# Seven products for both halves of the down projection, with weight sums added by DMA and results added to x from PSUM

## The chip, the cores and the metric

One Trainium2 chip, one of its cores. The time is that of one execution on the device, in microseconds (us); lower is better. Three executions of the kernel before took 1492.73, 1492.98 and 1493.35 us, median 1492.98 us.

## What is computed

The layer takes 256 tokens of width 2048 in float32. The change touches its MLP only:

```python
hm = rmsnorm(x, g_mlp[i])
x = x + jnp.square(jax.nn.relu(hm @ w_up[i])) @ w_down[i]
```

`w_up` is 2048 x 8192 and `w_down` is 8192 x 2048. Ahead of the MLP stand the input projections, two attention branches and an output projection; behind it stands a gated embedding with one more 2048 x 2048 product.

## The kernel before

**Precision.** Every weight tile is split into a high part `wh` (written by ACT, L82) and a low part `wl` (the rest, by DVE, L83), both fp32r. One split pair covers 128x1024 numbers. A product of an activation part and a weight chunk is three matmuls: high by high, high by low, low by high. In the up projection the weights are the stationary operand and both parts of the activations stream past them, so a step there is one matmul of 512 columns for `wh` and one of 256 for `wl` (L526, L527).

**The MLP's stages.** The hidden width is cut into eight slabs of 1024. `up_units` makes the hidden activations of one slab (eight 1 MB loads, each two split pairs, four calls of `hidden`). While it makes slab s + 1, the down projection of slab s runs beside it. `together` interleaves the streams of units: it gives each unit of a stream a due place between 0 and 1 and takes them in that order. A scheduler then orders the instructions on each engine; each engine runs its own in that order and waits at the first that isn't ready.

**The down projection.** For a slab, `w_down` is two halves `n` of the output columns, and each half is four quarters `(i, j)` of 512 rows by 512 columns, 1 MB each. Rows of tokens come in two tiles `tt` of 128. `plain_units` (half 1 of slabs 0 to 6, both halves of slab 7) forms the 2 x 2 block product with eight block products: four quarters, each split once (8 split pairs), 96 matmuls of 512 columns, collected in PSUM banks `m` and added to x by `add_rows` (L448). `fast_units` (half 0 of slabs 0 to 6) uses seven block products of sums (Strassen's scheme in Winograd's form): the sums of activations are made in `hidden` (L508 to L511), the sums of weights on DVE over the loaded quarters (L560, 128x2048), each of the seven products splits its own weights (14 split pairs) and needs 84 matmuls (L546, L548, L550) into banks `s`. Three partial results are copied out of PSUM by ACT (`keep`, L556) and added to x later (L560, L614); the rest go by `add_rows`. x itself lives in SBUF as `xr`.

**Buffers and queues.** `raw` (loads), `wh` and `wl` have three buffers each. The quarters of a fast half have four buffers of their own (`quart`). All weight loads are issued by SP (SyncE), in order; each waits there for its buffer. POOL (GpSimd) has no work in the MLP. `later(us, fn)` puts off an emission until the planner's clock, which `advance` moves, has gone on by so much.

Of the kernel before, what the change touches and what calls it, by code (L numbers as in the profile page):

```python
# [22 lines left out]
DH = 128  # L23
# [36 lines left out]
def layer_kernel(ctx: ExitStack, tc: tile.TileContext, xt, xm, pt, gains, qkg, cst,  # L60
                 wa, wba, wbb, wo, wup, wdn, wpg, wpp, out):
    nc = tc.nc
    const = ctx.enter_context(tc.tile_pool(name="const", bufs=1))
# [4 lines left out]
    work = mixers.enter_context(tc.tile_pool(name="work", bufs=2))  # L68
# [43 lines left out]
    def later(us, fn, *args):  # L112

        pending.append((clock[0] + us, len(pending), fn, args))
# [47 lines left out]

    cs = work.tile([P, C_END], F32, tag="cs", name="cs", bufs=1)
    idt = const.tile([P, P], F32, name="idt")
    gq = const.tile([P, 2, DH], F32, name="gq")
    ident = idt
    ones = cs[:, C_ONES:C_ONES + P]
    tri = cs[:, C_TRI:C_TRI + P]
# [53 lines left out]
    PIECE = 512  # L222
    xr = []
# [54 lines left out]
    for n, (dst, gain) in enumerate(((qT, gq[:, 0, :]), (kT, gq[:, 1, :]))):  # L278
        for g in range(2):
            if rt is None:  # L280
                ps = group_m(range(4), h, first_weights)
# [107 lines left out]

    yb = new_acts("yb", NH)  # L390
    sb_pair = []
    tri_r = const.tile([P, P], F32R, name="tri_r")
    ones_r = const.tile([P, P], F32R, name="ones_r")
    nc.scalar.activation(tri_r, tri, AF.Copy)
    nc.scalar.activation(ones_r, ones, AF.Copy)
    ga = [block([P, D], F32, f"ga{tt}") for tt in range(2)]
# [10 lines left out]
    for g in range(4):  # L407
        ps = group_m([wba[g, c] for c in range(2)], ya)
# [66 lines left out]

    rms = []
    r2 = const.tile([P, 2], F32, name="r2")
    r2n = const.tile([P, 1], F32, name="r2n")

    def mlp_norm():  # L480
        rms.append(rows_norm(ss1, "rt1", mw))
        nc.vector.tensor_tensor(r2, rms[0], rms[0], op=ALU.mult)
        nc.vector.tensor_scalar(r2n, r2[:, 0:1], -1.0, None, op0=ALU.mult)

    later(14, mlp_norm)
    mlp = ExitStack()
    hid = mlp.enter_context(tc.tile_pool(name="hid", bufs=7))
    mw = mlp.enter_context(tc.tile_pool(name="mw", bufs=2))
    ps2 = mlp.enter_context(tc.tile_pool(name="ps2", bufs=1, space=PSUM))
    FAST = [(s, 0) for s in range(7)]  # L490

    def bank2(tag, bufs=1):
        return ps2.tile([P, 512], F32, tag=tag, name=f"ps_{tag}", bufs=bufs)
# [44 lines left out]
    def fast_units(s, n, f):  # L538

        def product(ps, a, b, start):
            for p0 in range(2):
                for i, (wh, wl) in enumerate(split_weights(b[:, 2 * p0:2 * p0 + 2, :], 2, PIECE)):
                    k = 2 * p0 + i
                    nc.tensor.matmul(ps, f[k][:, 0, a, :], wh, start=start and k == 0, stop=False,  # L546
                                     skip_group_check=not start)
                    nc.tensor.matmul(ps, f[k][:, 0, a, :], wl, start=False, stop=False,  # L548
                                     skip_group_check=not start)
                    nc.tensor.matmul(ps, f[k][:, 1, a, :], wh, start=False, stop=k == 3,  # L550
                                     skip_group_check=not start)
                    advance(0.68)

        def keep(ps, tt):
            t = mw.tile([P, PIECE], F32, tag="cp", name="cp", bufs=5)
            nc.scalar.activation(t, ps, AF.Copy, scale=r2[:, tt:tt + 1])  # L556
            return t

        def add(a, b):
            nc.vector.tensor_tensor(a, a, b, op=ALU.add)  # L560

        b = {}
        for i, j in ((0, 0), (0, 1), (1, 1), (1, 0)):
            b[i, j] = mw.tile([P, 4, PIECE], F32, tag="quart", name="quart", bufs=4)
            nc.sync.dma_start(b[i, j].rearrange("p k c -> p (k c)"), wdn[s, n, i, j])
        c1, c2 = 2 * n * PIECE, (2 * n + 1) * PIECE
        left = [slice(c1, c1 + PIECE), slice(c2, c2 + PIECE)]
        waiting = []

        def sum_later(a, b):  # L570

            waiting.append((a, b))
            later(2, sums)

        def sums():
            while waiting:
                add(*waiting.pop(0))

        px = bank2("s", 4)
        product(px, A11, b[0, 0], True)  # L580
        s1 = keep(px, 1)
        sum_later(b[0, 0], b[0, 1])
        yield
        sums()
        pz = bank2("s", 4)
        product(pz, S1, b[0, 0], True)
        z0 = keep(pz, 0)
        sum_later(b[0, 0], b[1, 1])
        yield
        sums()  # L590
        product(px, S2, b[0, 0], False)
        s2 = keep(px, 1)
        sum_later(b[0, 0], b[1, 0])
        yield
        sums()
        pw = bank2("s", 4)
        product(pw, A22, b[0, 0], True)
        w0 = keep(pw, 0)
        sum_later(b[0, 1], b[1, 1])
        yield  # L600
        py = bank2("s", 4)
        product(py, A12, b[1, 0], True)
        add(xr[1][:, left[0]], s1)
        add_rows(1, c1, py, r2[:, 1:2])
        yield
        sums()
        product(px, S3, b[0, 1], False)
        add(xr[0][:, left[0]], w0)
        add_rows(0, c1, px, r2[:, 0:1])
        add(xr[0][:, left[1]], z0)  # L610
        add_rows(0, c2, px, r2n)
        yield
        product(pz, S4, b[1, 1], False)
        nc.vector.tensor_tensor(xr[1][:, left[1]], xr[1][:, left[1]], s2, op=ALU.subtract)  # L614
        add_rows(1, c2, pz, r2[:, 1:2])
        yield

    def plain_units(s, n, u):
# [33 lines left out]
    em = []  # L652

    def embedding_units():
        em.extend(mw.tile([P, D], F32, tag="quart", name=f"em{tt}", bufs=4) for tt in range(2))
        praw = mw.tile([P, 2, T], F32, tag="hs", name="praw", bufs=2)
        nc.sync.dma_start(praw, pt)
        pr = hid.tile([P, 2, 2, T], F32R, tag="hid", name="pr")
        split(pr[:, 0], pr[:, 1], praw)
        for n in range(2):  # L660
            raw = load(wpp[n], 2, 1024)
            for j in range(2):
                ps = [bank2("mm", 2) for _ in range(2)]
                parts = split_weights(raw[:, :, j * PIECE:(j + 1) * PIECE], 2, PIECE)
                for kt, (wh, wl) in enumerate(parts):
                    for tt in range(2):
                        t = slice(tt * P, (tt + 1) * P)
# [12 lines left out]
    def finished(g):  # L680
        if g == 0:
            h3.extend(new_acts("h3_", pool=blk))
        for tt in range(2):
            squares_rows(tt, g, ss2, mw.tile([P, PIECE], F32, tag="cp", name="junk", bufs=5))
        later(3, turn, g, h3, 2)

    def last_units(u):
# [8 lines left out]
    for s in range(7):  # L696
        hids.append([])
        streams = [(0.5, 16, up_units(s + 1, hids[s + 1]))]
        for n in range(2):
            if (s, n) in FAST:  # L700
                streams.append((0.3, 7, fast_units(s, n, hids[s])))
            else:
                streams.append((0.75, 8, plain_units(s, n, hids[s])))
        together(*streams)
# [4 lines left out]
    def gate_out(g, tt, ps, c0, n):  # L709

        a, c = g * PIECE + c0, slice(g * PIECE + c0, g * PIECE + c0 + n)
        o = mw.tile([P, n], F32, tag="cp", name="o", bufs=5)
        nc.scalar.activation(o, ps[:, c0:c0 + n], AF.Sigmoid, scale=rms[1][:, tt:tt + 1])
        nc.vector.tensor_tensor(o, o, em[tt][:, c], op=ALU.mult)
        nc.vector.tensor_tensor(o, o, xr[tt][:, c], op=ALU.add)
        nc.sync.dma_start(out[tt, :, c], o)
# [78 lines left out]
```

## Time and profile before

| | |
|---|---|
| median of 3 runs | 1492.98 us |
| the profiled execution, its own time | 1492.93 us |
| its span in the profile | 1491.1 us |
| slabs 0 to 6 with their down projections | about 716 to 1338 us of the span |
| PE busy, share of the span | 99% |
| DVE / ACT busy, share of the span | 67% / 56% |
| POOL busy | 42.4 us, all ahead of the MLP |
| read from DRAM | 275.83 MB |

The profiled execution is within 0.05 us of the median. In the profile, a row of the timeline gives the start in us from the span's start, the duration, the engine, the line, the operation and its tiles; "x2" is two of them merged; in brackets stands how long the engine was idle ahead of it and what ended that. Ends of matmuls are modelled, so the distance between starts is the better measure of a matmul's cost.

### The profile page before, as it was taken

The numbers are of one execution on the slowest core, as the hardware profiler recorded it, in microseconds if no ns is written. First come the engines' busy times: TensorE is split into PE (matmuls) and PEld (weight loads), VectorE is DVE, ScalarE is ACT, GpSimd is POOL, SyncE is SP. The second block draws the span as 40 slices with busy tenths as digits, with TensorE's granted clock in tenths as the row PEclk, the third lists the DMA queues.
The fourth block names the chain that finished last, engine by engine and source line by source line (L and its number), as shares of the span: only waits on it lengthen the run. The fifth ranks groups of instructions, "written<-read, shape, count | busy, mean of one in ns | idle before, by whom it ended". The sixth has DMA issues, their size and how long they took to land.

```text
span 1491.1 us, 17831 instructions
## 1 busy us (share of the span) xinstructions
PE 1470.8 (99%) x6960; PEld 1210.2 (81%) x6960; DVE 1000.4 (67%) x1209; ACT 840.3 (56%) x1084; POOL 42.4 (3%) x60
## 2 busy tenths in 40 slices
PE   7999999999999999999999999999999999999998
PEld 5888888888888888888787887878888787878886
DVE  5775555456555555556878879788787878765654
ACT  7444555488834444546655656656565655656543
POOL 0442000000000000000000000000000000000000
PEclk9999999999999999999999999999999999999999
DMA  8555544544455555557455464645546465444563
GB/s 330 174 196 193 175 155 159 194 169 170 169 182 190 193 185 186 194 178 302 141 198 198 170 226 140 228 170 191 204 155 239 143 208 191 159 146 154 201 221 111
DMA packets 40549, 279.09 MB, mean 187 GB/s; under 512 B 4624, under 2 KB 5136, under 8 KB 7312
## 3 DMA queue, kind: packets, MB, share of 16 engines
q1 hardware_dynamic: 40320, 277.92, 53.5%
q8 instruction: 54, 0.88, 0.2%
q14 instruction: 31, 0.25, 0.0%
q10 hardware_dynamic: 144, 0.02, 0.0%
HBM read 275.83 MB, written 2.10 MB: 186 GB/s over the span
## 4 chain that ended last, share of the span: by engine, by line
PE 92%; DVE 3%; issue 2%; DMA 1%; ACT 1%; SPq 0%; DVEq 0%; ACTq 0%
PE ps_mm L137 13%; PE ps_mm L139 13%; PE ps_mm L526 13%; PE ps_mm L138 13%; PE ps_mm L527 7%; PE ps_m L629 4%; PE ps_m L630 4%; PE ps_m L628 3%; PE ps_s L548 3%; PE ps_s L546 2%; PE ps_s L550 2%; PE ps_s L526 2%; DVE wl L83 2%; DMA raw<-in_wa 1%; ACT wh L82 1%
## 5 line engine op out<-in xcount | busy, mean ns | idle before, releaser
L83 DVE TENSOR_TENSOR wl<-raw,wh 128x1024 fp32r<-128x1024 f32 (+1 forms) x462 | 563.5, 1228 | 341.3 <-ACT wh L82 337.8
L82 ACT ACTIVATE wh<-raw 128x1024 fp32r<-128x1024 f32 (+1 forms) x462 | 485.3, 1054 | 404.2 <-PE ps_mm L139 222.8
L526 PE MATMUL ps_mm<-h,wh 128*128 128x512 f32 x896 | 321.3, 398 | 0.0
L137 PE MATMUL ps_mm<-wh,h 128*128 128x512 f32 x640 | 255.8, 400 | 5.5 <-ACT wh L82 5.5
L527 PE MATMUL ps_mm<-h,wl 128*128 128x256 f32 x896 | 251.8, 281 | 0.4
L138 PE MATMUL ps_mm<-wl,h 128*128 128x512 f32 x640 | 251.2, 393 | 0.6 <-DVE wl L83 0.5
L139 PE MATMUL ps_mm<-wh,h 128*128 128x512 f32 x640 | 251.0, 392 | 0.0
L526 PEld LDWEIGHTS ps_mm<-h,wh 128*128 128x128 f32 x896 | 168.3, 188 | 40.8 <-ACT wh L82 2.3
L83 DVE TENSOR_TENSOR wl<-quart,wh 128x1024 fp32r<-128x1024 f32 x98 | 120.1, 1225 | 83.3 <-ACT wh L82 83.2
L527 PEld LDWEIGHTS ps_mm<-h,wl 128*128 128x128 f32 x896 | 169.0, 189 | 8.2 <-DVE wl L83 3.2
L82 ACT ACTIVATE wh<-quart 128x1024 fp32r<-128x1024 f32 x98 | 104.0, 1061 | 123.2 <-PE ps_mm L526 87.0
L137 PEld LDWEIGHTS ps_mm<-wh,h 128*128 128x128 f32 x640 | 121.0, 189 | 31.7 <-ACT wh L82 8.1
L138 PEld LDWEIGHTS ps_mm<-wl,h 128*128 128x128 f32 x640 | 121.3, 189 | 26.8 <-DVE wl L83 2.6
L139 PEld LDWEIGHTS ps_mm<-wh,h 128*128 128x128 f32 x640 | 121.0, 189 | 25.8
L629 PE MATMUL ps_m<-wl,u 128*128 128x512 f32 x256 | 101.8, 397 | 4.1 <-DVE wl L83 4.0
L630 PE MATMUL ps_m<-wh,u 128*128 128x512 f32 x256 | 100.0, 391 | 0.0
L628 PE MATMUL ps_m<-wh,u 128*128 128x512 f32 x256 | 97.9, 392 | 1.6 <-DVE xr L448 1.6
L548 PE MATMUL ps_s<-wl,u 128*128 128x512 f32 x196 | 80.2, 409 | 0.0
L546 PE MATMUL ps_s<-wh,u 128*128 128x512 f32 x196 | 78.6, 401 | 0.0
L550 PE MATMUL ps_s<-wh,u 128*128 128x512 f32 x196 | 76.7, 392 | 0.0
L560 DVE TENSOR_TENSOR quart<-quart 128x2048 f32<-128x2048 f32 x28 | 64.1, 2289 | 0.5
L629 PEld LDWEIGHTS ps_m<-wl,u 128*128 128x128 f32 x256 | 48.1, 188 | 18.1 <-DVE wl L83 9.2
(204 smaller groups left out, 1826.0 us busy)
## 6 DMA issues: line engine op xcount, KB each, us to landing
raw<-in_wa SPq DMA_DIRECT2D x79, 1024.0 KB, 4.8
raw<-in_wup SPq DMA_DIRECT2D x64, 1024.0 KB, 4.8
raw<-in_wdn SPq DMA_DIRECT2D x36, 1024.0 KB, 4.8
quart<-in_wdn SPq DMA_DIRECT2D x28, 1024.0 KB, 4.8
raw<-in_wo SPq DMA_DIRECT2D x16, 1024.0 KB, 4.8
raw<-in_wpg SPq DMA_DIRECT2D x16, 1024.0 KB, 4.8
raw<-in_wba SPq DMA_DIRECT2D x8, 1024.0 KB, 4.8
raw<-in_wbb SPq DMA_DIRECT2D x8, 1024.0 KB, 4.8
```

Of the source, the lines that this page charges most:

```text
L82: nc.scalar.activation(hi, src, AF.Copy)
L83: nc.vector.tensor_tensor(lo, src, hi.bitcast(F32), op=ALU.subtract)
L137: nc.tensor.matmul(ps[tt], lhs[kt][:, 0, t], wh, start=kt == 0, stop=False)
L138: nc.tensor.matmul(ps[tt], lhs[kt][:, 0, t], wl, start=False, stop=False)
L139: nc.tensor.matmul(ps[tt], lhs[kt][:, 1, t], wh, start=False, stop=kt == last)
L526: nc.tensor.matmul(ps, wh, flat(h2[kt]), start=kt == 0, stop=False)
L527: nc.tensor.matmul(ps[:, :T], wl, h2[kt][:, 0, :], start=False, stop=kt == DT - 1)
L546: nc.tensor.matmul(ps, f[k][:, 0, a, :], wh, start=start and k == 0, stop=False, skip_group_check=not start)
L548: nc.tensor.matmul(ps, f[k][:, 0, a, :], wl, start=False, stop=False, skip_group_check=not start)
L628: nc.tensor.matmul(ps[tt], u[k][:, 0, a, :], wh, start=i + k == 0, stop=False)
L629: nc.tensor.matmul(ps[tt], u[k][:, 0, a, :], wl, start=False, stop=False)
L630: nc.tensor.matmul(ps[tt], u[k][:, 1, a, :], wh, start=False, stop=last)
```

## The change

- Half 1 of slabs 0 to 6 is also done by `fast_units`, so all 14 halves of these slabs take seven products. The two halves' streams stand at places 0.25 and 0.75 of a unit.
- In `fast_units` a half has one tile `chain` (three buffers) that holds quarter (0,0) and then grows by (0,1), (1,1) and (1,0). The first two sums are made by an accumulating DMA from DRAM that POOL issues (`add_loaded`, two DMAs of 512 KB per sum); the third is a DVE sum with a freshly loaded quarter (`last_sum`). A tile `right` (two buffers) holds (0,1) and gets (1,1) added on DVE. The two products with a plain quarter load it into `raw`.
- The order of the products is new. Nothing is copied out of PSUM: each product's bank is added to x by `add_rows` straight from PSUM, eight times per half, put off by 0.6 (once 2.1) on the planner's clock. Two of the seven products use banks `m`.
- Space: `gq`, `tri_r` and `ones_r` move to a pool that is closed ahead of the MLP; `cp` goes from five to two buffers and serves scratch and the last output only; the embedding's tiles `em` use the buffers of `right`.

```diff
-    r2n = const.tile([P, 1], F32, name="r2n")
+    r2n = const.tile([P, 2], F32, name="r2n")
...
-    FAST = [(s, 0) for s in range(7)]
+    FAST = [(s, n) for s in range(7) for n in range(2)]
...
-        def keep(ps, tt):
-            t = mw.tile([P, PIECE], F32, tag="cp", name="cp", bufs=5)
-            nc.scalar.activation(t, ps, AF.Copy, scale=r2[:, tt:tt + 1])
-            return t
+        def quarter(tag, bufs, i, j):
+            q = mw.tile([P, 4, PIECE], F32, tag=tag, name=tag, bufs=bufs)
+            nc.sync.dma_start(q.rearrange("p k c -> p (k c)"), wdn[s, n, i, j])
+            return q
+
+        def add_loaded(q, i, j):
+
+            for k in range(0, 4, 2):
+                nc.gpsimd.dma_start(q[:, k:k + 2, :].rearrange("p k c -> p (k c)"),
+                                    wdn[s, n, i, j, :, k * PIECE:(k + 2) * PIECE],
+                                    accum_op=ALU.add)
...
+        def last_sum():
+            add(chain, load(wdn[s, n, 1, 0], 4, PIECE))
...
+        chain = quarter("chain", 3, 0, 0)
         px = bank2("s", 4)
-        product(px, A11, b[0, 0], True)
-        s1 = keep(px, 1)
-        sum_later(b[0, 0], b[0, 1])
+        product(px, A11, chain, True)
+        add_loaded(chain, 0, 1)
+        later(0.6, add_rows, 1, c1, px, r2[:, 1:2])
         yield
-        sums()
+        py = bank2("m", 2)
+        product(py, A12, load(wdn[s, n, 1, 0], 4, PIECE), True)
+        later(0.6, add_rows, 1, c1, py, r2[:, 1:2])
+        yield
         pz = bank2("s", 4)
-        product(pz, S1, b[0, 0], True)
-        z0 = keep(pz, 0)
-        sum_later(b[0, 0], b[1, 1])
+        product(pz, S1, chain, True)
+        add_loaded(chain, 1, 1)
+        later(0.6, add_rows, 0, c2, pz, r2[:, 0:1])
+        right = quarter("right", 2, 0, 1)
         yield
...
+        b11 = load(wdn[s, n, 1, 1], 4, PIECE)
+        product(pz, S4, b11, False)
+        later(0.6, add_rows, 1, c2, pz, r2[:, 1:2])
+        later(2, add, right, b11)
         yield
...
+        product(px, S2, chain, False)
+        later(0.6, add_rows, 1, c2, px, r2n[:, 1:2])
+        later(6, last_sum)
         yield
...
+        pw = bank2("m", 2)
+        product(pw, A22, chain, True)
+        later(0.6, add_rows, 0, c1, pw, r2[:, 0:1])
         yield
...
+        product(px, S3, right, False)
+        later(0.6, add_rows, 0, c1, px, r2[:, 0:1])
+        later(2.1, add_rows, 0, c2, px, r2n[:, 0:1])
         yield
...
-                streams.append((0.3, 7, fast_units(s, n, hids[s])))
+                streams.append((0.25 + 0.5 * n, 7, fast_units(s, n, hids[s])))
```

How the order moves, first on DVE, in the middle of a slab, at a weight sum. Before, a sum (L560) of two loaded quarters stands between the splits of one product and those of the next (`quart_6979` is quarter (0,0), `cp` a copied result):

```order
L83 TENSOR_TENSOR wl_7093<-quart_6979,wh_7092 128x1024
L560 TENSOR_TENSOR quart_6979<-quart_6979,quart_6983 128x2048
L83 TENSOR_TENSOR wl_7151<-raw_7148,wh_7150 128x1024
L83 TENSOR_TENSOR wl_7155<-raw_7148,wh_7154 128x1024
L83 TENSOR_TENSOR wl_7175<-quart_6979,wh_7174 128x1024
L533 TENSOR_TENSOR hs_6951<-ps_mm_7054,ev_7121 128x256
L560 TENSOR_TENSOR xr0_247<-xr0_247,cp_7102 128x512
```

With the change (L568 is the sum, `raw_7171` the load of a product with a plain quarter, `raw_7320` quarter (1,1), which is loaded into the buffer that `raw_7171` had):

```order
L83 TENSOR_TENSOR wl_7184<-raw_7171,wh_7183 128x1024
L83 TENSOR_TENSOR wl_7198<-raw_7195,wh_7197 128x1024
L533 TENSOR_TENSOR hs_6991<-ps_mm_7089,ev_7157 128x256
L83 TENSOR_TENSOR wl_7202<-raw_7195,wh_7201 128x1024
L448 SCALAR_TENSOR_TENSOR xr1_248<-ps_m_7170,r2_5040,xr1_248 128x512
L83 TENSOR_TENSOR wl_7224<-chain_7019,wh_7223 128x1024
L508 TENSOR_TENSOR hr_7161<-hr_7161 128x128
L509 TENSOR_TENSOR hr_7161<-hr_7161 128x128
L568 TENSOR_TENSOR right_7245<-right_7245,raw_7320 128x2048
```

The sum now reads a tile whose load starts seven rows earlier, and an addition from PSUM (L448) stands among the splits.

The second place is SP's queue of loads in the same slab. Before, loads of the up projection (`in_wup`) stand with those of the plain half and of the four `quart` tiles:

```order
L91 DMA raw_7381<-in_wdn 128x2048
L91 DMA raw_7427<-in_wup 128x2048
L565 DMA quart_7707<-in_wdn 128x2048
L91 DMA raw_7520<-in_wup 128x2048
L91 DMA raw_7565<-in_wdn 128x2048
L565 DMA quart_7709<-in_wdn 128x2048
```

With the change, from the load of `raw_7171` to that of `raw_7582`; the tiles of L91 share three buffers in this order:

```order
L91 DMA raw_7171<-in_wdn 128x2048
L91 DMA raw_7195<-in_wup 128x2048
L91 DMA raw_7293<-in_wup 128x2048
L91 DMA raw_7320<-in_wdn 128x2048
L91 DMA raw_7375<-in_wup 128x2048
L91 DMA raw_7401<-in_wdn 128x2048
L91 DMA raw_7465<-in_wup 128x2048
L91 DMA raw_7516<-in_wdn 128x2048
L91 DMA raw_7568<-in_wup 128x2048
L91 DMA raw_7582<-in_wdn 128x2048
```

Where `quart` tiles with buffers of their own stood, quarters now go through the three `raw` buffers, alternating with the up projection's loads.

## Rows read from the trace of the kernel before

**Rows 1.** The page: busy time of each engine, and TensorE's granted clock in 40 slices.

```profile
PE 1470.8 (99%) x6960; PEld 1210.2 (81%) x6960; DVE 1000.4 (67%) x1209; ACT 840.3 (56%) x1084; POOL 42.4 (3%) x60
...
PEclk9999999999999999999999999999999999999999
```

**Rows 2.** Timeline of DVE: the same instruction in two neighbouring slabs.

```profile
810.06 0.29 DVE L510 TENSOR_TENSOR hr<-hr 128x128 f32<-128x128 f32 x1
...
898.85 0.28 DVE L510 TENSOR_TENSOR hr<-hr 128x128 f32<-128x128 f32 x1
```

**Rows 3.** Timeline of PE: twelve 512-column matmuls in a row, then eight up-projection pairs.

```profile
1382.62 0.39 PE L628 MATMUL ps_s<-wh,u 128*128 128x512 f32 x1
...
1385.34 0.39 PE L668 MATMUL ps_mm<-wh,pr 128*128 128x512 f32 x1
...
709.95 0.39 PE L526 MATMUL ps_s<-h,wh 128*128 128x512 f32 x1
712.72 0.39 PE L526 MATMUL ps_s<-h,wh 128*128 128x512 f32 x1
```

**Rows 4.** Timeline of DVE, 810 to 825 us: a dense stretch with two weight sums.

```profile
810.26 2.29 DVE L560 TENSOR_TENSOR quart<-quart 128x2048 f32<-128x2048 f32 x1
812.46 0.29 DVE L511 TENSOR_TENSOR hr<-hr 128x128 f32<-128x128 f32 x1
812.66 2.59 DVE L83 TENSOR_TENSOR wl<-raw,wh 128x1024 fp32r<-128x1024 f32 x2
815.17 1.22 DVE L83 TENSOR_TENSOR u<-hr,u 128x1024 fp32r<-128x1024 f32 x1
816.31 0.42 DVE L533 TENSOR_TENSOR hs<-ps_mm,ev 128x256 f32<-128x256 f32 x1
816.64 2.28 DVE L560 TENSOR_TENSOR quart<-quart 128x2048 f32<-128x2048 f32 x1
818.84 2.36 DVE L83 TENSOR_TENSOR wl<-raw,wh 128x1024 fp32r<-128x1024 f32 x2
821.11 0.69 DVE L560 TENSOR_TENSOR xr<-xr,cp 128x512 f32<-128x512 f32 x1
821.71 1.22 DVE L83 TENSOR_TENSOR wl<-quart,wh 128x1024 fp32r<-128x1024 f32 x1
...
849.18 1.40 DVE L448 SCALAR_TENSOR_TENSOR xr<-ps_m,r,xr 128x512 f32<-128x512 f32 x2
850.50 2.35 DVE L83 TENSOR_TENSOR wl<-raw,wh 128x1024 fp32r<-128x1024 f32 x2
```

**Rows 5.** Busy time by window: a stage ahead, one slab, and a dense stretch.

```profile
670.00:716.00 46.00, 46.00 (x267) 40.24 (x268) 31.22 (x51) 28.73 (x43) 0.00 (x0) 1.00 0.73 272
808.95:897.74 88.79, 88.26 (x438) 72.15 (x437) 72.42 (x83) 52.33 (x62) 0.00 (x0) 1.00 0.54 190
1075.57:1110.30 34.73, 34.26 (x167) 27.31 (x166) 32.70 (x33) 20.26 (x24) 0.00 (x0) 1.00 0.37 129
```

**Rows 6.** Waits, 690 to 1250 us: who waited for whom, total us, times, longest.

```profile
DVE wl L83 <- ACT wh L82: 103.4, 108, 1.6
...
ACT cp L556 <- PE ps_s L550: 20.4, 17, 1.9
...
PE ps_m L629 <- DVE wl L83: 3.6, 6, 1.2
```

**Rows 7.** DMA issues, 670 to 716 us: size and median us from issue to landing.

```profile
raw<-in_wup SPq DMA_DIRECT2D x7, 1024.0 KB, 4.8
quart<-in_wdn SPq DMA_DIRECT2D x4, 1024.0 KB, 7.5
```

**Rows 8.** Timeline ahead of the MLP: POOL, and a DVE instruction with and without POOL busy.

```profile
88.25 2.15 POOL L259 TENSOR_TENSOR qn<-qn,gq 128x512 f32<-128x512 f32 x1 [9.96 <-DVE qn L258]
...
89.16 1.79 DVE L251 TENSOR_TENSOR qsq<-qraw 128x512 f32<-128x512 f32 x1
106.20 0.69 DVE L251 TENSOR_TENSOR qsq<-qraw 128x512 f32<-128x512 f32 x1 [0.44 <-ACT qraw L250]
```

More of the change, by code (lines that the diff above doesn't have):

```diff
@@ L164, in layer_kernel @@
     idt = const.tile([P, P], F32, name="idt")
-    gq = const.tile([P, 2, DH], F32, name="gq")
+    gq = work.tile([P, 2, DH], F32, tag="gq", name="gq", bufs=1)
     ident = idt
@@ L391, in layer_kernel @@
     sb_pair = []
-    tri_r = const.tile([P, P], F32R, name="tri_r")
-    ones_r = const.tile([P, P], F32R, name="ones_r")
+    tri_r = work.tile([P, P], F32R, tag="tri_r", name="tri_r", bufs=1)
+    ones_r = work.tile([P, P], F32R, tag="ones_r", name="ones_r", bufs=1)
     nc.scalar.activation(tri_r, tri, AF.Copy)
@@ L482, in mlp_norm @@
         nc.vector.tensor_tensor(r2, rms[0], rms[0], op=ALU.mult)
-        nc.vector.tensor_scalar(r2n, r2[:, 0:1], -1.0, None, op0=ALU.mult)
+        nc.vector.tensor_scalar(r2n, r2, -1.0, None, op0=ALU.mult)
     later(14, mlp_norm)
@@ L559, in add @@
         def add(a, b):
             nc.vector.tensor_tensor(a, a, b, op=ALU.add)
[L562 to L565, printed above, removed]
+        def last_sum():
+            add(chain, load(wdn[s, n, 1, 0], 4, PIECE))
         c1, c2 = 2 * n * PIECE, (2 * n + 1) * PIECE
-        left = [slice(c1, c1 + PIECE), slice(c2, c2 + PIECE)]
@@ L568, in fast_units @@
[L568 to L577, printed above, removed]
+        chain = quarter("chain", 3, 0, 0)
         px = bank2("s", 4)
-        product(px, A11, b[0, 0], True)
-        s1 = keep(px, 1)
-        sum_later(b[0, 0], b[0, 1])
+        product(px, A11, chain, True)
+        add_loaded(chain, 0, 1)
+        later(0.6, add_rows, 1, c1, px, r2[:, 1:2])
@@ L583, in fast_units @@
         yield
-        sums()
+        py = bank2("m", 2)
+        product(py, A12, load(wdn[s, n, 1, 0], 4, PIECE), True)
+        later(0.6, add_rows, 1, c1, py, r2[:, 1:2])
+        yield
         pz = bank2("s", 4)
-        product(pz, S1, b[0, 0], True)
-        z0 = keep(pz, 0)
-        sum_later(b[0, 0], b[1, 1])
+        product(pz, S1, chain, True)
+        add_loaded(chain, 1, 1)
+        later(0.6, add_rows, 0, c2, pz, r2[:, 0:1])
+        right = quarter("right", 2, 0, 1)
         yield
-        sums()
@@ L591, in fast_units @@
-        product(px, S2, b[0, 0], False)
-        s2 = keep(px, 1)
-        sum_later(b[0, 0], b[1, 0])
+        b11 = load(wdn[s, n, 1, 1], 4, PIECE)
+        product(pz, S4, b11, False)
+        later(0.6, add_rows, 1, c2, pz, r2[:, 1:2])
+        later(2, add, right, b11)
         yield
[L595 to L599, printed above, removed]
+        product(px, S2, chain, False)
+        later(0.6, add_rows, 1, c2, px, r2n[:, 1:2])
@@ L600, in fast_units @@
+        later(6, last_sum)
         yield
[L601 to L604, printed above, removed]
+        pw = bank2("m", 2)
+        product(pw, A22, chain, True)
+        later(0.6, add_rows, 0, c1, pw, r2[:, 0:1])
         yield
[L606 to L615, printed above, removed]
+        product(px, S3, right, False)
+        later(0.6, add_rows, 0, c1, px, r2[:, 0:1])
+        later(2.1, add_rows, 0, c2, px, r2n[:, 0:1])
         yield
@@ L654, in embedding_units @@
     def embedding_units():
-        em.extend(mw.tile([P, D], F32, tag="quart", name=f"em{tt}", bufs=4) for tt in range(2))
+        em.extend(mw.tile([P, D], F32, tag="right", name=f"em{tt}", bufs=2) for tt in range(2))
         praw = mw.tile([P, 2, T], F32, tag="hs", name="praw", bufs=2)
@@ L683, in finished @@
         for tt in range(2):
-            squares_rows(tt, g, ss2, mw.tile([P, PIECE], F32, tag="cp", name="junk", bufs=5))
+            squares_rows(tt, g, ss2, mw.tile([P, PIECE], F32, tag="cp", name="junk", bufs=2))
         later(3, turn, g, h3, 2)
@@ L711, in gate_out @@
         a, c = g * PIECE + c0, slice(g * PIECE + c0, g * PIECE + c0 + n)
-        o = mw.tile([P, n], F32, tag="cp", name="o", bufs=5)
+        o = mw.tile([P, n], F32, tag="cp", name="o", bufs=2)
         nc.scalar.activation(o, ps[:, c0:c0 + n], AF.Sigmoid, scale=rms[1][:, tt:tt + 1])
```

## The prediction

> **What bounds the kernel now.** I began with the page. TensorE (PE) is busy 99% of the span, DVE 67%, and the granted clock is at its upper level, 2.4 GHz, in all 40 slices [rows 1]. That says "PE", but a busy PE here includes modelled ends, so I went to the stage that the change touches and took distances between starts. The timeline of DVE shows the same instruction of two neighbouring slabs at 810.06 and 898.85 us: one slab takes 88.8 us [rows 2]. The timeline of PE gives the price of its work when nothing holds it up: twelve 512-column matmuls from 1382.62 to 1385.34, 0.2267 us each, and eight pairs of 512 and 256 columns from 709.95 to 712.72, 0.346 us a pair [rows 3]. A slab has 128 pairs (8 loads of 16 chunks), 84 matmuls of the fast half and 96 of the plain one: 128 x 0.346 + 180 x 0.2267 = 44.3 + 40.8 = 85.1 us. So PE loses 3.7 us of a slab, although the page calls it full.
>
> The windows then show who is near behind. In a slab DVE is busy 72.4 of 88.8 us, and in the stretch from 1075.57 to 1110.30 us, 32.70 of 34.73, which is 94% [rows 5]. The waits say what DVE idles for: `wl` waits for ACT's `wh`, 103.4 us over six slabs, and PE in turn stands 3.6 us for `wl` at L629 [rows 6]. The reader should see two engines, one with 85.1 us of work, the other with about 70, tied together by three buffers of split weights.
>
> **PE's part.** Seven plain halves of 96 matmuls become fast halves of 84: 7 x 12 x 0.2267 = 19.0 us less. A slab is then 44.3 + 168 x 0.2267 = 82.4 us of PE work.
>
> **DVE's part.** I price its instructions by distances between starts in dense stretches [rows 4]: a split 1.135 us (two from 818.84 to 821.11), a weight sum 2.20, an addition to x from SBUF 0.60, one from PSUM 0.66 (two from 849.18 to 850.50), a split of `u` 1.14, a 128-column sum 0.20, an L533 0.33. A slab before has 38 splits (16 for the up projection, 14 fast, 8 plain), 4 weight sums, 4 additions from SBUF and 8 from PSUM, four times `hidden` (1.14 + 4 x 0.20) and 8 of L533:
> 43.1 + 8.8 + 2.4 + 5.3 + 7.8 + 2.6 = 70.0 us.
> Six more split pairs come with the second fast half. The weight sums on DVE stay at 4 (two per half, the other two go to DMA). The 12 additions become 16, all from PSUM:
> 49.9 + 8.8 + 10.6 + 7.8 + 2.6 = 79.7 us.
> So DVE goes from 82% of PE's work to 97% of it. This is what the forecast hangs on: **PE's work falls by 2.7 us a slab and DVE's rises by 9.7.** The gain of 19.0 us comes only as far as DVE keeps up.
>
> **ACT** gets six splits more and loses four copies of PSUM (L556). Even at the 1.135 us of a split on DVE six are 6.8 us, on 52.3 busy [rows 5]: under 60 of at least 82, beside other work all of it, so I cost it at nothing; with less than 82 us of other work it would show one for one. The copies' waits for PE (20.4 us over six slabs [rows 6]), behind which the next `wh` stood, go; an L448 that isn't ready now holds the next `wl` on DVE instead. No row prices that. The put-off of 0.6 covers part; I leave it inside the idle share below.
>
> **Loads.** Before, a slab loads 16 tiles of 1 MB. Now a fast half takes five loads through SP and two through POOL's accumulation (quarters (1,0), (0,1) and (1,1) come twice), so a slab takes 22, and the rate goes from 190 to 22 x 1.049 / 87 = 265 GB/s. The stage from 670 to 716 us moved 272 GB/s at a DMA share of 0.73 while PE was busy for 46.00 of 46 us [rows 5], so the rate as such is carried. An accumulation also reads its target; no row has one. Its bounds are nothing and as much again, 4 of 22 tiles; I take it as a plain load and leave the rest to the landing times below.
>
> What is late next is a tile that DVE waits for in order. In the order with the change three of the four DVE sums of a slab read a tile whose `raw` buffer came free shortly ahead. `raw_7320` takes the buffer of `raw_7171`; between that one's last split and the sum stand three splits, an L533, an L448 and two 128-column sums, 4.8 us. For `raw_7401` it is four splits and two L448, 5.9 us; for `raw_7582` three splits, an L448 and another sum, 6.3 us. Issue to landing took a median of 4.8 us for the up projection's loads and 7.5 us for four tiles asked for close together [rows 7]. At 4.8 none of the three is late; at 7.5 all are, by 2.7, 1.6 and 1.2, together 5.5 us. Loads asked for singly and close together both occur in a slab now (`raw_7401` is asked for right behind four accumulations of 512 KB), so I take half-way, 2.7 us a slab. Both ends, 0 and 5.5, go into the range. The accumulations themselves have about 16 us of DVE work between the last split of the old tile and the first of the new, so they cost nothing unless one takes over twice the longer landing.
>
> A rule of the Trainium skill speaks against the change here: "DMA: Bandwidth & Descriptors", section "Issuing engines are not separate DMA queues", says that DMAs started from different engines run on the same 16 DMA engines and interleave. By it every tile that POOL asks for lengthens SP's beside it, and the sum would take 5.5 where I take 2.7, a slab of 90.1 us. The trace has no POOL transfer beside SP's, but its close loads at 7.5 us [rows 7] agree with it.
>
> **The sum.** From PE's side: 82.4 us and the 3.7 us lost today make 86.1. From DVE's side: 79.7 us at the dense stretch's share of 94.2% make 84.6, and with 2.7 for late tiles 87.3. The longer one counts: 87.3 us a slab, 1.5 less than 88.8, seven times: 10.5 us. The profiled execution took 1492.93 us, within 0.05 of the median, so I forecast **1482 us**. Everything outside the seven slabs has the same instructions; the shorter supply of `cp` buffers at the end meets outputs that leave a whole group of products apart, and I put it at nothing.
>
> **Rivals.**
> *Full gain.* DVE's idle shrinks further since the copies on ACT are gone, and half of PE's 3.7 us goes too. The slab is then 84.6 us (DVE's bound) and the time 1492.9 - 7 x 4.2 = 1464 us. For it: ACT's 20.4 us. Against: DVE at 97% of PE's work never was so dense over a whole slab. Chance 0.12.
> *A draw.* DVE's idle comes to 9.1 us a slab, which is 88.8 - 79.7, and eats the gain: 1490 to 1496 us. Chance 0.12.
> *Slower, by DVE waiting in order for loaded tiles.* Place: the three sums at L568, with the splits queued behind them. Price: 5.5 us a slab at 7.5 us to landing, hence 84.6 + 5.5 = 90.1 us and 1493 + 9 = 1502 us; each further us of landing adds 3 us a slab, 21 us in all. It decides from 9.1 us of DVE idle a slab on. For it: the margins of 4.8 to 6.3 us against 7.5, and the higher rate. Against: most loads of the busiest stage landed in 4.8 us [rows 7]. Chance 0.20, most of it from 1496 to 1503 us.
> *Slower, by POOL standing in DVE's way.* Ahead of the MLP a DVE instruction with two SBUF inputs took 1.79 us beside a POOL instruction and 0.69 without, 1.10 more [rows 8]. If each of POOL's 8 DMA issues in a slab did that to a split, DVE would have 8.8 us more, 93 us or more a slab, and the time would be above 1522 us. Against: those POOL instructions read tensors; a DMA issue doesn't. Chance 0.06.
> On this the Trainium skill, "SBUF — State Buffer", section "Who interferes with whom", holds that a VectorE instruction with two SBUF inputs collides with GpSimd only where GpSimd reads SBUF, and that writing descriptors needs the write side. By the row alone the sum would rise by up to 7 x 8.8 = 62 us, by the rule by nothing; no run here shows yet which.
>
> **How the numbers follow.** A measurement of this kernel can tell about 0.2%, 3 us, from no change. The forecast's own case (1470 to 1490 us) has 0.50. With the full gain, faster has 0.62; the draw 0.12; slower 0.20 + 0.06 = 0.26. The range, 1466 to 1503 us, leaves out part of the full gain below, and above it the POOL case and the tail of the late tiles, together some 0.2.
>
> **What would show it.** Right: slabs of 86 to 88 us; PE with 84 fewer 512-column matmuls; DVE busy above 90% of a slab; DVE idle ahead of L568 by DMA of 2 to 3 us a slab; few waits of `wl` for `wh`. Wrong: slabs of 84 to 85 us (DVE wasn't the bound), DVE idle above 9 us a slab, or splits that take over 1.3 us where POOL issues.

## The result, and the profile after

The changed kernel took 1502.25 us (median of four runs, 1498.81 to 1503.90); the kernel before took 1493.16 us beside it. The ratio is 1.0058 [1.0040, 1.0076]: slower by 0.6%, where 1482 us was forecast. The profiled execution of the changed kernel is the shortest of the four, 1498.81 us with a span of 1497.0.

The page of the changed kernel, engines and DMA queues (packets, MB, share of 16 engines), beside [rows 1]:

```profile
PE 1457.7 (97%) x6876; PEld 1193.9 (80%) x6876; DVE 1066.7 (71%) x1279; ACT 868.4 (58%) x1098; POOL 91.5 (6%) x116
...
q1 hardware_dynamic: 42336, 292.60, 54.9%
q0 software_dynamic: 8064, 29.36, 10.9%
```

PE has its 84 instructions less, DVE's busy time rose by 66 us, and a second queue carries the accumulations.

The timeline of DVE, the same instruction of two neighbouring slabs, answers to [rows 2]:

```profile
808.38 0.29 DVE L508 TENSOR_TENSOR hr<-hr 128x128 f32<-128x128 f32 x1 [0.23 <-ACT hr L504]
...
899.74 0.29 DVE L508 TENSOR_TENSOR hr<-hr 128x128 f32<-128x128 f32 x1 [0.24 <-ACT hr L504]
```

This slab took 91.4 us. Over five slabs (808.38 to 1260.22) the mean is 90.4, 1.5 more than the 88.9 of the same five slabs before (808.19 to 1252.71); seven times 1.5 is 10 us. The whole stage says the same: from its first to its last up-projection matmul the changed kernel took 676.3 us where it took 666.1, 10.2 more. Ahead of this stage and behind it the profiled execution is 1.4 and 2.9 us shorter than before's, so that its span is 5.9 us longer. So the loss sits in slabs 0 to 6, and each slab has 82.4 us of PE work in 90.4 us. **PE stands for 8.0 us a slab where it stood for 3.8** (3.7 in the one slab of [rows 2]). The work went down as planned; the stalls ate it, and more.

Whose fault the stalls are, the waits say (690 to 1250 us; total, times, longest). Changed kernel, beside [rows 6]:

```profile
ACT wh L82 <- PE ps_mm L526: 69.7, 62, 2.0
ACT wh L82 <- PE ps_s L551: 65.3, 75, 1.9
DVE wl L83 <- ACT wh L82: 50.2, 75, 2.4
...
PEld ps_s L549 <- DVE wl L83: 20.1, 30, 1.1
...
ACT wh L82 <- DMA raw<-in_wup: 9.1, 5, 2.6
...
DVE right L568 <- DMA raw<-in_wdn: 1.1, 1, 1.1
```

Read them as a ring. DVE waits for ACT's `wh`, ACT waits until PE gives a `wh` buffer back, PE waits for DVE's `wl`. DVE is idle for some 9 us a slab and still the one that PE mostly waits for. The last line is the wait that the forecast had feared: 1.1 us in six slabs.

Where PE stands longest shows the timeline of the changed kernel around 870 us, DVE first:

```profile
866.61 2.28 DVE L568 TENSOR_TENSOR chain<-chain,raw 128x2048 f32<-128x2048 f32 x1
868.81 2.52 DVE L83 TENSOR_TENSOR wl<-chain,wh 128x1024 fp32r<-128x1024 f32 x2
871.25 2.28 DVE L568 TENSOR_TENSOR chain<-chain,raw 128x2048 f32<-128x2048 f32 x1
873.45 0.74 DVE L448 SCALAR_TENSOR_TENSOR xr<-ps_s,r2n,xr 128x512 f32<-128x512 f32 x1
874.11 0.41 DVE L533 TENSOR_TENSOR hs<-ps_mm,ev 128x256 f32<-128x256 f32 x1
874.44 1.21 DVE L83 TENSOR_TENSOR wl<-chain,wh 128x1024 fp32r<-128x1024 f32 x1
```

Then ACT and PE in the same microseconds:

```profile
863.81 1.06 ACT L82 ACTIVATE wh<-chain 128x1024 fp32r<-128x1024 f32 x1 [1.42 <-PE ps_s L551]
866.60 1.06 ACT L82 ACTIVATE wh<-chain 128x1024 fp32r<-128x1024 f32 x1 [1.73 <-PE ps_mm L526]
869.00 1.06 ACT L82 ACTIVATE wh<-chain 128x1024 fp32r<-128x1024 f32 x1 [1.34 <-DVE chain L568]
871.75 1.06 ACT L82 ACTIVATE wh<-chain 128x1024 fp32r<-128x1024 f32 x1 [1.69 <-PE ps_s L551]
```
```profile
874.08 0.50 PE L526 MATMUL ps_mm<-h,wh 128*128 128x512 f32 x1 [0.27 <-ACT wh L82]
875.71 0.50 PE L549 MATMUL ps_m<-wl,u 128*128 128x512 f32 x1 [1.13 <-DVE wl L83]
```

From 871.25 to 874.44 DVE makes no split: a weight sum, an addition from PSUM and an L533 stand in its queue. PE runs out of `wl` and waits until 875.71. The same stall comes back in every slab (782.75, 874.08, 963.72, 1054.48 us and so on). DVE's rows follow each other without a gap here. ACT stood at 863.81, 866.60 and 871.75 because all `wh` buffers were in use, and at 869.00 for the sum itself, but DVE waited for none of it: at this place DVE's own queue is late.

An earlier place in a slab shows how an engine with idle time can come late; DVE, ACT and then PE:

```profile
936.24 1.23 DVE L83 TENSOR_TENSOR wl<-raw,wh 128x1024 fp32r<-128x1024 f32 x1 [0.97 <-ACT wh L82]
937.96 1.23 DVE L83 TENSOR_TENSOR wl<-raw,wh 128x1024 fp32r<-128x1024 f32 x1 [0.50 <-ACT wh L82]
```
```profile
935.14 1.06 ACT L82 ACTIVATE wh<-raw 128x1024 fp32r<-128x1024 f32 x1 [1.31 <-PE ps_mm L526]
936.87 1.06 ACT L82 ACTIVATE wh<-raw 128x1024 fp32r<-128x1024 f32 x1 [0.67 <-PE ps_s L551]
```
```profile
951.94 0.50 PE L549 MATMUL ps_s<-wl,u 128*128 128x512 f32 x1 [0.58 <-DVE wl L83]
```

DVE stands because ACT stands, and ACT because PE hasn't given back a `wh` buffer. Behind that come a sum and several additions, and some 15 us later PE waits for DVE.

To put one number on it, I took every distance between starts on PE from 716 to 1340 us, less the price of the instruction from [rows 3] (0.2267 us for 512 columns, 0.119 for 256, the rest of a pair). A matmul missing from the trace counts as a stall in this, of 0.23 us if it is a single one of 512 columns, so I count the larger ones alone. Excesses of 0.3 us and more: 8 with 6.9 us before, 48 with 33.2 us in the changed kernel.

The windows from 716 to 1340 us (PE, PEld, DVE, ACT, POOL busy; clock; DMA share; GB/s), before and then changed:

```profile
716.00:1340.00 624.00, 617.95 (x3052) 504.70 (x3050) 503.02 (x563) 366.45 (x437) 0.00 (x0) 1.00 0.53 183
```
```profile
716.00:1340.00 624.00, 600.06 (x2934) 484.81 (x2933) 563.61 (x627) 389.48 (x444) 48.43 (x56) 1.00 0.82 250
```

### The profile page after: what moved, and what is told of

Same layout as the page of the kernel before. It is cut to its first block, busy times and chain, and to the rows that moved or that the text cites. A ratio compares the mean times of both kernels' runs of the same rounds, so it can differ in the third digit from the quotient of the medians.

```text
span 1497.0 us, 17950 instructions
## 1 busy us (share of the span) xinstructions
PE 1457.7 (97%) x6876; PEld 1193.9 (80%) x6876; DVE 1066.7 (71%) x1279; ACT 868.4 (58%) x1098; POOL 91.5 (6%) x116
## 4 chain that ended last, share of the span: by engine, by line
PE 80%; DVE 10%; DMA 5%; ACT 3%; issue 3%; SPq 0%; DVEq 0%; ACTq 0%
PE ps_mm L139 13%; PE ps_mm L138 13%; PE ps_mm L137 13%; PE ps_mm L526 9%; DVE wl L83 5%; PE ps_mm L527 5%; PE ps_s L549 3%; PE ps_s L551 3%; PE ps_s L547 2%; DMA raw<-in_wup 2%; ACT wh L82 2%; PE ps_s L526 2%; DMA raw<-in_wa 1%; PE ps_m L549 1%; DMA raw<-in_wdn 1%
## 5 line engine op out<-in xcount | busy, mean ns | idle before, releaser
L526 PE MATMUL ps_mm<-h,wh 128*128 128x512 f32 x896 | 324.8, 398 | 3.8 <-ACT wh L82 3.8
L82 ACT ACTIVATE wh<-chain 128x1024 fp32r<-128x1024 f32 x112 | 118.3, 1056 | 84.9 <-PE ps_s L551 33.2
L83 DVE TENSOR_TENSOR wl<-chain,wh 128x1024 fp32r<-128x1024 f32 x112 | 136.2, 1217 | 8.9 <-ACT wh L82 8.4
L549 PE MATMUL ps_s<-wl,u 128*128 128x512 f32 x280 | 113.9, 407 | 10.0 <-DVE wl L83 9.9
L563 POOL DMA_DIRECT2D chain<-in_wdn x56 | 48.4, 865 | 1120.4 <-DVE hs L533 594.8
L547 PE MATMUL ps_s<-wh,u 128*128 128x512 f32 x280 | 110.6, 395 | 0.2 <-ACT wh L82 0.2
L551 PE MATMUL ps_s<-wh,u 128*128 128x512 f32 x280 | 110.5, 395 | 0.0
L549 PEld LDWEIGHTS ps_s<-wl,u 128*128 128x128 f32 x280 | 52.5, 188 | 31.2 <-DVE wl L83 22.2
L547 PEld LDWEIGHTS ps_s<-wh,u 128*128 128x128 f32 x280 | 52.6, 188 | 13.3 <-ACT wh L82 1.0
L551 PEld LDWEIGHTS ps_s<-wh,u 128*128 128x128 f32 x280 | 52.6, 188 | 10.7 <-DVE u L83 1.4
L549 PE MATMUL ps_m<-wl,u 128*128 128x512 f32 x112 | 45.4, 405 | 7.7 <-DVE wl L83 7.7
```

The lines of the kernel that those rows point to most:

```text
L82: nc.scalar.activation(hi, src, AF.Copy)
L83: nc.vector.tensor_tensor(lo, src, hi.bitcast(F32), op=ALU.subtract)
L526: nc.tensor.matmul(ps, wh, flat(h2[kt]), start=kt == 0, stop=False)
L563: nc.gpsimd.dma_start(q[:, k:k + 2, :].rearrange("p k c -> p (k c)"), wdn[s, n, i, j, :, k * PIECE:(k + 2) * PIECE], accum_op=ALU.add)
```

## The experiments

My first theories were A, that DVE's own work sets the pace, and B, that the accumulating DMAs disturb the loads.

**Without the accumulations.** Both `add_loaded` calls are left out; every other instruction stands in the same order.

```diff
-        add_loaded(chain, 0, 1)
...
-        add_loaded(chain, 1, 1)
```

> Leaves out the 56 accumulating DMAs of the changed kernel (so two of four weight sums are missing); DVE, ACT and PE keep their instructions. Theory A (DVE, with 79.7 us of work per slab in its own order and three buffers of split weights, sets the pace): 1490 to 1500 us, within 6 us of the changed kernel. Theory B (POOL's transfers delay SP's loads and DVE or ACT wait for them): 1482 us or less, since the slabs then get to PE's 82.4 us and today's 3.7 us of stalls.

Measured: 1496.00 us, ratio to before 1.0022 [1.0012, 1.0031]. The 56 accumulations cost some 6 us. The DMA issues of the page show what they did to the loads: this kernel, then the changed one.

```profile
raw<-in_wup SPq DMA_DIRECT2D x64, 1024.0 KB, 4.8
```
```profile
raw<-in_wup SPq DMA_DIRECT2D x64, 1024.0 KB, 5.2
```

The waits of `wh` for `raw<-in_wup` (9.1 us above) are gone without them. That leaves most of the changed kernel's stalls: B explains the smaller part.

**Half of the additions left out.**

```diff
-        later(0.6, add_rows, 1, c1, px, r2[:, 1:2])
...
-        later(0.6, add_rows, 0, c2, pz, r2[:, 0:1])
...
-        later(0.6, add_rows, 1, c2, px, r2n[:, 1:2])
...
-        later(0.6, add_rows, 0, c1, pw, r2[:, 0:1])
```

> Leaves out four of the eight additions to x per fast half: 56 instructions of 0.66 us on DVE, 5.3 us per slab, 37 us in all; all transfers, splits and products stay. Theory A: most of it comes off the time until PE sets the pace: 1465 to 1478 us. Theory B: DVE's work is not what ends late, so 1495 to 1502 us.

Measured: 1514.88 us, 1.0141 [1.0114, 1.0169]. Less work, slower, against both theories. The scheduler had put the instructions of PE, DVE and ACT into another order, in which a sum does come up ahead of its load's landing, as this line of the waits shows:

```profile
DVE right L568 <- DMA raw<-in_wdn: 15.7, 8, 2.7
```

How much of the time is the order's, the run can't say. So a kernel that leaves something out is a new order too, and tells nothing of the thing left out alone. That set the method of the later runs.

**The new form for half 0 alone.**

```diff
-    FAST = [(s, n) for s in range(7) for n in range(2)]
+    FAST = [(s, 0) for s in range(7)]
...
-                streams.append((0.25 + 0.5 * n, 7, fast_units(s, n, hids[s])))
+                streams.append((0.3, 7, fast_units(s, n, hids[s])))
```

> Only half 0 of slabs 0 to 6 in the new form (chain, accumulating DMA, additions from PSUM), half 1 plain as before. PE has the 85.1 us of before per slab, DVE 38 splits, 2 sums, 12 additions from PSUM and the rest: 65.8 us, 4.2 fewer than before. Theory A: stalls fall below the 3.7 us of before: 1480 to 1490 us. Theory B: half the added transfers, 19 tiles per slab: 1493 to 1498 us.

Measured: 1719.57 us, 1.1506 [1.1464, 1.1547], far outside what was expected. The waits show PE and ACT stopping each other for much longer than in the changed kernel:

```profile
ACT wh L82 <- PE ps_mm L526: 137.2, 60, 5.6
ACT wh L82 <- PE ps_m L620: 85.5, 24, 6.0
```

and the timeline of PE what follows from it:

```profile
1102.07 0.49 PE L526 MATMUL ps_mm<-h,wh 128*128 128x512 f32 x1 [1.55 <-ACT wh L82]
1103.58 0.58 PE L527 MATMUL ps_mm<-h,wl 128*128 128x256 f32 x1 [1.02 <-DVE wl L83]
1103.96 0.63 PE L526 MATMUL ps_mm<-h,wh 128*128 128x512 f32 x1
1104.39 0.41 PE L527 MATMUL ps_mm<-h,wl 128*128 128x256 f32 x1
```

Behind two waits a 512-column matmul takes 0.43 us between starts, against 0.2267 in [rows 3]; from 1105 to 1107 us the granted clock is 0.51, the level of 1.2 GHz, where from 1101 to 1103 it was 1.00. So part of this time is the clock's, and the run can't price half of the change. I draw nothing from it for that.

**Four buffers.** `wh` and `wl` get four buffers, paid for with one of `chain`.

```diff
-            wh = wts.tile([P, n, cols], F32R, tag="wh", name="wh")
-            wl = wts.tile([P, n, cols], F32R, tag="wl", name="wl")
+            wh = wts.tile([P, n, cols], F32R, tag="wh", name="wh", bufs=4)
+            wl = wts.tile([P, n, cols], F32R, tag="wl", name="wl", bufs=4)
...
-        chain = quarter("chain", 3, 0, 0)
+        chain = quarter("chain", 2, 0, 0)
```

> The changed kernel with four buffers each of wh and wl in place of three (the space comes from chain, two buffers in place of three). Theory A in its sharper form (DVE loses time where it is a whole buffer ahead and PE where it is behind; the depth of the buffers ties them): 1480 to 1492 us. Theory A without that (DVE's work alone): 1497 to 1502. Theory B: no change or slower, 1497 to 1505 us, as the chain's load now starts later.

Measured: 1489.80 us, 0.9981 [0.9969, 0.9992], 12 us less than the changed kernel. But the order had changed again, on PE too.

**With the order held.** From here on, extra ordering constraints, which wait for nothing, tie the engines to the changed kernel's order, and one thing differs at a time. First, DVE's work, taken out in 16 thin slices or in four lumps:

```diff
+        def add_few(tt, c0, ps, scale):
+            c = slice(c0, c0 + 8)
+            nc.vector.scalar_tensor_tensor(xr[tt][:, c], ps[:, :8], scale, xr[tt][:, c],
+                                           op0=ALU.mult, op1=ALU.add)
...
-        later(0.6, add_rows, 1, c1, px, r2[:, 1:2])
+        later(0.6, add_few, 1, c1, px, r2[:, 1:2])
```

(and so at all eight additions of a half), and in the other kernel

```diff
         def add(a, b):
+            a, b = a[:, :, :2], b[:, :, :2]
             nc.vector.tensor_tensor(a, a, b, op=ALU.add)
```

> Every engine issues the changed kernel's instructions in the changed kernel's order; only the 16 additions to x of each slab 0 to 6 that come straight from PSUM write 8 of their 512 columns, so their sums are left out of the other 504. By the 0.66 us of a full one in rows 4 and about 0.12 us for a narrow one, an estimate from the 0.20 us of a 128-column row there, that takes some 8.5 us of the vector engine's 81 busy us out of a slab, spread over 16 places. Theory A, the vector engine's own work sets the pace (it is busy 81 of the 90.4 us of a slab and waits in lockstep for the rest): the slab falls to between 86 and 88.5 us, bounded below by TensorE's 82.4 us of work and the 3.7 us of stalls that it kept before; 7 slabs give 1470 to 1490 us. Rival B, the order of the instructions and the three buffers of wh and wl set it, whatever an addition costs: within 5 us of the changed kernel's 1502.

> The same held order; only the four sums of weight quarters that the vector engine does in each slab 0 to 6 (2.28 us each) touch 2 columns of each of the four chunks, so the weights of the other columns are left unsummed. That takes some 8.5 to 8.8 us out of the vector engine's slab, the same as with the narrow additions, but in four lumps. Theory A, total work: the same fall as there, 1470 to 1490 us. Theory A', the lumps count (behind a sum of 2.28 us the splits stand still for longer than the three buffers cover, behind an addition of 0.66 us they do not): this falls clearly further than the narrow additions do, by over 8 us. Rival B, order and buffers alone: within 5 us of 1502.

Measured: 1492.44 us, 0.9996 [0.9987, 1.0006], and 1492.27 us, 0.9995 [0.9985, 1.0006]. Ten us each: between theory A (12 to 32 less) and B (5 at most), and no difference between slices and lumps, which takes A' away. In the windows of the second,

```profile
716.00:1340.00 624.00, 609.73 (x2983) 492.69 (x2982) 515.19 (x633) 396.33 (x450) 48.55 (x56) 1.00 0.83 252
```

DVE is nearly back at before's 503.02. A slab takes 88.8 us, so 8.3 us less of DVE's work brought 1.6. PE still stalls for 6.4 us a slab, and the kernel has only drawn level with before. **DVE's work is not the whole of it.** It is most of the stall at the pair of sums: with narrow sums PE loses 0.42 us there (at 874.07) where it lost 1.40 (at 874.08).

Second, the buffers, with a control that has the `chain` change alone:

> TensorE, the vector engine and ScalarE issue the changed kernel's instructions in the changed kernel's order; wh and wl have four buffers in place of three, chain two in place of three (only the order of the loads on SP moves, since a chain tile comes free later). Theory C1, the depth of wh and wl: with three buffers a tile has some 3 us of cover (three times 2.72 us of TensorE's work on a tile, less the 2.72 us of its own use, the cast and the split), which a weight sum and an addition from PSUM (2.28 and 0.66 us) behind each other use up; with four the cover is over 5 us, so most of the 55 us of TensorE's stalls in slabs 0 to 6 go: 1475 to 1490 us, at least as good as the 1490 of the run with four buffers and its own order. Theory C2, the order: the 12 us of that run came from the other order on TensorE, and the buffers alone do little: 1496 to 1504 us.

> The control for the run with four buffers in held order: the same, with three buffers for wh and wl and two for chain. All theories: only the loads on SP differ from the changed kernel's, 1500 to 1506 us; if the late loads of chain cost anything it is more than 1506, and the four buffers are then to be measured from here.

Measured: 1485.14 us, 0.9953 [0.9936, 0.9971], with four buffers; the control 1502.51 us, 1.0063 [1.0048, 1.0078], as long as the changed kernel, so neither the constraints nor the third `chain` buffer matter. Same order of PE, DVE and ACT, and of the loads too, one more buffer each for `wh` and `wl`: **17 us.** Where DVE stood twice at 936 to 938 us above, it makes three splits in a row with four buffers:

```profile
927.94 3.48 DVE L83 TENSOR_TENSOR wl<-raw,wh 128x1024 fp32r<-128x1024 f32 x3
```

Of the stall that PE had at 951.94 and at that place of every slab (some 0.75 us) 0.38 or less is left. The waits show the ring loosened (65.3, 69.7 and 50.2 us in the changed kernel):

```profile
ACT wh L82 <- PE ps_s L551: 28.5, 47, 1.2
ACT wh L82 <- PE ps_mm L526: 26.0, 18, 2.0
...
DVE wl L83 <- ACT wh L82: 15.7, 17, 1.6
```

Other waits took part of their place: ACT now stands 24.7 us for DVE's sum at `chain` (8.1 in the changed kernel) and 18.4 us for `raw<-in_wdn` (1.3).

Theory C1 (depth) holds against C2 (order). One detail of it does not. The expectation had a sum and an addition behind each other as what four buffers cover; yet at the pair of sums PE still waits once a slab, 1.54 us where it was 1.13. ACT's next cast there reads the sum itself and waits for it, however many buffers are free:

```profile
863.65 2.01 ACT L82 ACTIVATE wh<-chain 128x1024 fp32r<-128x1024 f32 x2 [4.11 <-DVE chain L568]
```
```profile
870.36 0.50 PE L549 MATMUL ps_m<-wl,u 128*128 128x512 f32 x1 [1.54 <-DVE wl L83]
```

The expectation's cover was also worked out with 2.72 us of PE's work for every tile; that is what a split pair of a plain half feeds (12 matmuls). In a fast half a pair feeds 6, 1.36 us, in the up projection eight pairs of matmuls, 2.77 us. What went are the smaller stalls: those of 0.3 us and more fell from 51 with 36.6 us in the control to 26 with 23.7 us.

Third, both together:

> Four buffers for wh and wl, held order as in the run above, and the four sums of weight quarters that the vector engine does in a slab touch 2 columns of each chunk, so the other columns are left unsummed (8.5 us of its time a slab; with three buffers this was worth 10 us of 1502). Theory C1 with A, the two add up because the lag of the vector engine is what the buffers cover: at least 10 us below the four buffers with the full sums, 1465 to 1478 us, the floor being 1464. Rival, four buffers cover the lag already: the full sums cost nothing any more, within 4 us of the four buffers with full sums.

Measured: 1470.68 us, 0.9844 [0.9830, 0.9859], 14.5 us below the four buffers with full sums.

```profile
716.00:1340.00 624.00, 618.84 (x3069) 511.05 (x3068) 522.64 (x645) 404.75 (x469) 47.42 (x55) 1.00 0.84 259
```

A slab takes 86.0 us (803.17 to 1232.96 us, five slabs), PE's 82.4 and 3.6 of stalls. The four runs as a table, us of the whole kernel and us of a slab:

| | three buffers | four buffers |
|---|---|---|
| DVE's sums whole | 1502.3, 90.4 | 1485.1, 88.0 |
| DVE's sums narrow | 1492.3, 88.8 | 1470.7, 86.0 |

Each of the two helps more when the other is there too: neither does the other's work. Why they add to each other is not shown.

**Two versions for use.** The third sum by accumulating DMA as well, A22's product last and onto the bank `px`, which saves an addition per half; once with the buffers of the changed kernel, once with four and two.

```diff
-        later(6, last_sum)
-        yield
-        pw = bank2("m", 2)
-        product(pw, A22, chain, True)
-        later(0.6, add_rows, 0, c1, pw, r2[:, 0:1])
+        add_loaded(chain, 1, 0)
         yield
         product(px, S3, right, False)
+        later(0.6, add_rows, 0, c2, px, r2n[:, 0:1])
+        yield
+        product(px, A22, chain, False)
         later(0.6, add_rows, 0, c1, px, r2[:, 0:1])
-        later(2.1, add_rows, 0, c2, px, r2n[:, 0:1])
```

> The same without the buffers: three for wh, wl and chain as in the changed kernel. Theory A: 5.9 us less of the vector engine's work in a slab, at half to all of it, bounded by TensorE: 1472 to 1488 us. Rival B, buffers decide: within 5 us of 1502. Rival D, late transfers: 1500 us or more, with waits for chain.

> The changed kernel with four buffers each for wh and wl and two for chain, and two pieces of the vector engine's work taken out with the result kept: the last weight sum comes by an accumulating DMA (two more in each half), and the product of A22 runs last and adds onto the bank of the product before it, which saves one addition from PSUM in each half. By 2.28 and 0.66 us that is 5.9 us less of the vector engine's time in a slab. Theory A: the four buffers gave 12 us, and 5.9 us a slab at half to all of it are 20 to 35 us once the pace is the vector engine's: 1465 to 1480 us, not below the 1464 of the full gain. Rival D, the DMA engines (busy 82 to 83% of the stretch with four accumulations in a slab; the two more bring about 6.5 points) deliver late: 1488 us or more, with waits for tiles raw and chain in place of the lockstep.

Measured: 1496.78 us, 1.0031 [1.0021, 1.0040], with three buffers: 5.9 us less of DVE's work a slab, in an order of its own, brought 5 us in all, at the edge of what B expected and far from A's 14 us or more. With four: **1476.51 us, 0.9890 [0.9875, 0.9905]**, 1.1% less than before and 26 us less than the changed kernel; it beats both. Its windows:

```profile
716.00:1340.00 624.00, 609.62 (x3038) 504.81 (x3037) 537.49 (x615) 400.05 (x466) 72.10 (x84) 1.00 0.90 257
```

The DMA engines are at 0.90, and the up projection's loads land in 6.1 us on that page, but `wh` waits for `raw` only 21.1 us in six slabs. Rival D didn't decide.

Was it its order? The last run gives this kernel the order of the one with three buffers:

> The kernel with the merged addition, the third accumulation and four buffers, with TensorE, the vector engine and ScalarE in the order of the same kernel with three buffers (1497 us); with its own order it took 1476.5. Theory C1, depth: within 4 us of 1476.5. Theory C2, order: within 4 us of 1497.

Measured: 1475.90 us, 0.9883 [0.9868, 0.9898]. Not the order: in the order of the kernel with three buffers, the change of buffers is worth 21 us.

## Why the prediction was wrong

- **PE's part was right.** 84 instructions fewer, 82.4 us of work a slab; 86.0 us a slab appeared where the ring was wide enough and DVE at its old load, next to the 86.1 that the sum had "from PE's side".
- **DVE's part was right.** 563.61 us busy of 624 is 81.6 of 90.4 us a slab; the sum had 79.7 by distances between starts. Where idle time follows, an instruction is busy for longer than that (a split 1.22 us, not 1.135).
- **ACT at nothing was right as work, wrong as a place.** It has 38% of the stretch free (389.48 of 624 us busy), but waits for `wh` buffers then and can't use that time to get ahead.
- **The step that failed** is the one in the sum, "79.7 us at the dense stretch's share of 94.2% make 84.6", with "The longer one counts". It took the slab for the larger of two engines' bounds. The 94.2% came from 35 us in which PE waited for `wl` once, for 0.47 us, and had plain-half tiles as well to work on; over whole slabs of the changed kernel DVE's 79.7 us are 88%. In a whole slab PE's work and the stalls add: 82.4 + 8.0. The stalls depend on DVE's lag and on how many tiles ACT and DVE may be ahead. The prediction had named "three buffers of split weights" and then given them no term. Measured, that term is 2.4 us a slab for one buffer more of each (17 us in all), and DVE's sums are worth 1.6 a slab with three buffers and 2.0 with four.
- **Why the buffers weigh more than before** I can only argue. A split pair of a plain half gives PE 12 matmuls (2.7 us), one of a fast half 6 (1.4 us), so three buffers are less time of cover than they were, and six more pairs a slab must pass. With DVE back near its old load the changed order still stalls for 6.4 us where before stood for 3.7, of which the accumulations (6 us over seven slabs) can be 0.9. The kernel before with four buffers wasn't run, so how much of the buffers' worth is the change's doing stays open.
- **Late tiles were mis-sized.** The 2.7 us a slab measured 0.2 (1.1 us in six slabs at `right`, none of note at `chain`): the loads of `raw<-in_wdn` landed in 4.9 us, near the lower of the two values of [rows 7], and I had gone half-way to the upper one. The trace of the kernel before could have told: the 7.5 us of [rows 7] are four loads ahead of the slabs, and from 716 to 1340 us its 24 `quart` loads landed in a median of 4.8 us. Loads were late at another place, ACT's casts (10.4 us in six slabs). The rival built on late sums forecast 1502 us, the time that came, by a mechanism that didn't take place; the range reached up to 1503 us for this rival, so that it held the time was luck. The rule on issuing engines that I had set beside it (the Trainium skill, "DMA: Bandwidth & Descriptors", section "Issuing engines are not separate DMA queues") agrees in direction: without POOL's transfers the up projection's loads landed 0.4 us earlier. But 6 us of the time went with them, where the sum by that rule had 5.5 us a slab, 38 in all. The close loads of [rows 7] were no evidence for it: SP had issued all of them.
- **The draw's mechanism was nearest.** It had DVE idle for 9.1 us a slab; 90.4 less 79.7 is 10.7.
- **POOL in DVE's way falls.** Of the 304 splits from 716 to 1340 us 41 overlap one of POOL's 56 issues of 0.86 us. They took a mean of 1217.5 ns, the other 263 one of 1219.0. The page of the profile has the splits of `chain` and POOL's issues:

```profile
L83 DVE TENSOR_TENSOR wl<-chain,wh 128x1024 fp32r<-128x1024 f32 x112 | 136.2, 1217 | 8.9 <-ACT wh L82 8.4
...
L563 POOL DMA_DIRECT2D chain<-in_wdn x56 | 48.4, 865 | 1120.4 <-DVE hs L533 594.8
```

  On this the trace agrees with the Trainium skill, "SBUF — State Buffer", section "Who interferes with whom", and not with the price taken from [rows 8].

## What to carry to other kernels

When a change takes work from the engine that bounds a kernel and makes its helpers busier, don't take the larger of two sums of work: give the buffers between them a term of their own. A producer that shows idle time and is waited for all the same may lack buffers as well as speed; here one more buffer of each kind was worth 17 us, a tenth of DVE's work 10. Look at each stall by itself, too: the one at the pair of sums went with the narrow sums and stayed with four buffers. And to price one part of a scheduled kernel, hold the order of the engines: a version with less work and a new order was 13 us slower.

## What the runs showed of the hardware

An accumulating DMA took the DMA engines about twice as long per byte as a load. In the changed kernel from 716 to 1340 us (queue, packets, MB, share of 16 engines):

```profile
q1 hardware_dynamic: 17425, 126.11, 55.4%
q0 software_dynamic: 8064, 29.36, 26.2%
```

That is 0.44% per MB for loads and 0.89% for accumulations; the prediction had taken them as plain loads and named the double as its bound. The size of the packets doesn't look like the reason: accumulations go in packets of 4 KB that took a mean of 362 ns, and 512 packets of 4 KB of plain loads ahead of the MLP took 169 ns. Whether it is the adding or POOL's queue, no run separates. The DMA share from 716 to 1340 us was 0.58 without accumulations, 0.82 with four sums a slab and 0.90 with six, in a kernel that still gained.

In the run with one half in the new form the granted clock fell to its lower level, 1.2 GHz, again and again: its mean was 0.83 to 0.93 in each 100 us from 700 to 1500 us. At the place shown PE had stood for 1.55 and 1.02 us just before, and the 512-column matmuls behind that took 0.43 us; a stall there cost more than its own length. In the other runs the clock was 0.99 or 1.00 from 716 to 1340 us.
